# Where VectorE and ScalarE do the work between two matmul jobs: the convolution's weight sums, the feed-forward's norm, retention's gates

## The chip, the cores and the metric

The kernel is one program on one core of one Trainium2 chip. It computes one inference step of a small two-layer decoder. The metric is the device time of one execution in microseconds (us); smaller is better. The engines are named as the profile names them: PE (TensorE, matrix products), PEld (its weight loads), DVE (VectorE), ACT (ScalarE), POOL (GpSimd) and SP (SyncE, which issues most of the loads).

## The reference

Two groups of tokens share all weights: a prompt of 512 tokens and 8 sample sequences of 4 tokens, together 544 columns. D_MODEL is 1024, D_FF is 2816. Layer 0 mixes with a short gated convolution, layer 1 with four heads of retention; each layer then has a feed-forward. All is float32.

```python
def rmsnorm(x, g):
    return x * rsqrt(mean(x * x) + RMS_EPS) * g

def swiglu(x, w_gate, w_up, w_down):
    return (silu(x @ w_gate) * (x @ w_up)) @ w_down

def short_conv_mixer(x, buf, w_in, w_conv, w_out):
    b, c, h = split(x @ w_in, 3)
    u = c * h
    full = concatenate([buf, u], axis=1)
    y = sum(w_conv[j] * full[:, j:j + L] for j in range(3))
    return (b * y) @ w_out, full[:, -2:]

def retention_mixer(x, s0, pos, w_in, gn_g, w_out):
    q, k, v, g = split(x @ w_in)
    o, S = retention_chunkwise(rotary(q, pos), rotary(k, pos) * 256 ** -0.5, v, s0)
    return (silu(g) * groupnorm(o) * gn_g) @ w_out, S

for i in range(2):
    x = x + mixer_i(rmsnorm(x, norm_mix[i]))
    x = x + swiglu(rmsnorm(x, norm_ffn[i]), w_gate[i], w_up[i], w_down[i])
y = rmsnorm(x, final_norm)
```

The outputs are y of both groups, the last two rows of the convolution's input, and the retention states S.

## The kernel before

**Operands.** Every float32 operand of a matmul is split into a high part and a low part of a narrower type: `split` makes the high part on ACT (L202) and the low part on DVE (L203). A product is high x high, high x low and low x high. Names show it: `wh` and `wl` are the parts of a weight, `h` and `l` those of a sum. The activations `x` lie with features on the 128 partitions and tokens along the row, 544 columns in two halves of 272 (`HT`).

**Jobs.** Where two blocks of outputs use the same activations, the kernel computes a 2 x 2 block product with seven products instead of eight (a Strassen scheme). One such unit is a `Job`. Its products run in the order 1, then 6, 5, 2 in some turn, then 7, 3, 4; each is 12 matmuls of 272 columns (four blocks of depth by three split products, L411; a feed-forward's `down` has three blocks). Products accumulate in PSUM banks `a`, `b`, `c`: 1, 6, 7 and 4 run on in the same bank `a`, so that between them the bank is read out: `summed` takes product 1 as "u1", 6 as "u2" and 5 as "p5" with copies on ACT (L514), and adds "c11", "u3" and "c12" on DVE (L516). The "u3" add, after product 7, is called the third sum. "c21", after product 4, is taken by the job's own function.

**Weights of a job.** `weights7` loads two weights of 128 x 1024 (tiles `w`, SP's queue) and makes from them four sums of 128 x 512 on DVE (L357 to L360: two into `w2`, one in place, one into `w4`). Then the parts: of the first and the third weight by `mixed` (ACT L333 high part, DVE L334 half of the low part, ACT L335 a negated copy into the other half, and a POOL DMA L336 that adds the weight to it from DRAM), of `w2` and `w4` by `split` (`h2`, `l2`, `h4`, `l4`). The tiles `w`, `wh` and `wl` come from pools of three, those of `w2` and `w4` from single ones; `cb` is one large buffer that serves as a second `w`.

**Order.** `run` goes through a list of jobs: it prepares the next job's weights in the code ahead of the current job's middle products, starts the next job's first product, and ends the current job. A scheduler merges the code into one row of instructions for each engine; `tc.issue_after(x)` gives an instruction a place behind x in the same engine's row. Each engine runs its row in order, so an instruction that waits holds all behind it. PSUM has two double banks (`mm`) and four single ones (`sm`) in these stages.

**The four places.** The convolution (`job`, run from L735) has jobs in turn for c, h and b of two feature blocks; its first pair is computed by plain products (L187) and is scaled by the norm's factors R in L677 before the jobs start. A feed-forward (`ffn`, called once for each layer) has jobs in pairs of gate and up; while its first two run, the norm's factor is made: five small matmuls (L274), DVE L249, POOL's power L252, five transposes on PE (L256) and copies into R on ACT (L285, L286). Gate's result is copied (L871), multiplied by R (DVE L872), goes through Silu (ACT L873) and is multiplied by R again. Retention's `gates` (run inside the first feed-forward's last part through `ahead`, 583 to 686 us) has eight gate jobs and three k jobs. A gate job ends in c21: a copy on ACT (L1168), a product with R on DVE (L1170), Silu on ACT (L1171), two scales on ACT (L1173), and a store of the tile to DRAM from ACT's queue (L1174). The tile is one of the four of tag "gu".

## Time and profile before

| | us |
|---|---|
| device time, three runs | 1387.44, 1388.99, 1385.43 |
| median | 1387.44 |
| profiled execution, its own time | 1386.94 |
| its span in the trace | 1385.2 |
| granted clock of TensorE, mean | 0.999 |

The profile names an instruction by its line, its engine, its operation and its tiles (output <- inputs, buffer numbers left out). A row of a timeline reads: start in us from the span's start, duration in us, engine, line, operation, out<-in, size, count, and in brackets the time for which the engine stood idle ahead of it, with what released it. The table of stretches gives for each window its length, and for each engine the busy time and the count of instructions, then the granted clock, the DMA share and the bytes moved. In the groups by tile three numbers in ns are the shortest, the median and the longest. PE's matmuls overlap, so the sum of busy times of neighbours is more than the time from start to start.

### The profile page before, as it was taken

Reading aid. Unit: us, or ns where it says so; the run is one execution under the profiler, and the core shown is the slowest. Engines: PE = TensorE matmul, PEld = TensorE weight load, DVE = VectorE, ACT = ScalarE, POOL = GpSimd, SP = SyncE. Lnnn points to the kernel's source line nnn. Section 1 sums busy time; section 2 is a strip of 40 time slices with the busy share of each in tenths; the row PEclk is TensorE's granted clock in tenths of the full one; section 3 lists DMA queues with packets and bytes.
Section 4 is the critical chain, followed back from the end, with each engine's and each line's share of the span. In section 5 each row is a group of like instructions: output and inputs, shape, how many; then the busy total and the mean of one; then the engine's idle time right before and its main releaser. Section 6 shows DMA issues by size and latency. Waiting matters only on the chain.

```text
span 1385.2 us, 26505 instructions
## 1 busy us (share of the span) xinstructions
PE 1375.7 (99%) x10420; PEld 1313.7 (95%) x10420; DVE 1134.0 (82%) x1929; ACT 822.9 (59%) x1288; POOL 217.8 (16%) x249
## 2 busy tenths in 40 slices
PE   9999999999999999999999999999999999999998
PEld 9999999999999999999978887887899999999997
DVE  6988889898989888777868586586799898989875
ACT  7666567667667656767641413224377767667654
POOL 0111011212222213211200000000112212221212
PEclk9999999999999999999999999999999999999999
DMA  6477347777777754777666455475756777777752
GB/s 224 115 162 169 109 107 162 176 169 179 151 184 154 165 126 123 201 175 221 187 230 228 149 186 201 136 261 183 220 131 157 171 176 173 155 178 166 165 111 88
DMA packets 99438, 232.89 MB, mean 168 GB/s; under 512 B 9809, under 2 KB 33889, under 8 KB 98929
## 3 DMA queue, kind: packets, MB, share of 16 engines
q1 hardware_dynamic: 68464, 167.26, 39.2%
q0 software_dynamic: 28400, 55.82, 23.4%
q10 hardware_dynamic: 2448, 8.12, 1.5%
q8 instruction: 81, 1.33, 0.4%
q14 instruction: 45, 0.36, 0.1%
HBM read 191.05 MB, written 28.42 MB: 158 GB/s over the span
## 4 chain that ended last, share of the span: by engine, by line
PE 94%; DVE 3%; ACT 1%; DMA 1%; issue 0%; POOL 0%; DVEq 0%; SPq 0%; POOLq 0%; ACTq 0%
PE sm L411 43%; PE mm L411 16%; PE mm L187 14%; PE sm L187 5%; PE sm L1344 2%; PE sm L1345 2%; PE sm L1346 2%; PE sm L175 2%; PE sm L176 1%; PE sm L177 1%; PE sm L1594 1%; DVE ol L203 1%; DMA w<-in_cvin_dram 1%; PE mm L1355 1%; PE mm L1612 1%; PE mm L1522 1%
## 5 line engine op out<-in xcount | busy, mean ns | idle before, releaser
L411 PE MATMUL sm<-oh,wh 128*128 128x272 f32 x856 | 247.2, 289 | 1.3 <-DVE h L516 1.3
L411 PE MATMUL sm<-ol,wh 128*128 128x272 f32 x856 | 246.2, 288 | 0.0
L411 PE MATMUL sm<-oh,wl 128*128 128x272 f32 x856 | 246.1, 288 | 0.0
L202 ACT ACTIVATE h<-w 128x512 fp32r<-128x512 f32 (+3 forms) x171 | 137.7, 805 | 85.8 <-PE mm L411 77.6
L203 DVE TENSOR_TENSOR l<-w,h 128x512 fp32r<-128x512 f32 (+3 forms) x171 | 154.6, 905 | 23.2 <-ACT h L202 21.0
L333 ACT ACTIVATE wh<-w 128x1024 fp32r<-128x1024 f32 (+1 forms) x133 | 132.9, 999 | 53.5 <-PE sm L411 43.4
L411 PEld LDWEIGHTS sm<-oh,wh 128*128 128x128 f32 x856 | 161.3, 188 | 1.9 <-DVE h L516 1.5
L411 PEld LDWEIGHTS sm<-oh,wl 128*128 128x128 f32 x856 | 161.0, 188 | 0.0
L411 PEld LDWEIGHTS sm<-ol,wh 128*128 128x128 f32 x856 | 160.8, 188 | 0.0
L202 ACT ACTIVATE wh<-w 128x1024 fp32r<-128x1024 f32 (+3 forms) x80 | 69.2, 874 | 123.7 <-PE mm L187 61.2
L411 PE MATMUL sm<-parts,wh 128*128 128x272 f32 x736 | 142.6, 288 | 0.0
L336 POOL DMA_DIRECT2D wl<-in_ffgu_dram x87 | 81.7, 939 | 320.5 <-ACT wl L335 136.0
L411 PEld LDWEIGHTS sm<-parts,wh 128*128 128x128 f32 x736 | 115.5, 188 | 0.0
L411 PE MATMUL mm<-oh,h 128*128 128x272 f32 x396 | 114.0, 288 | 0.0
L411 PE MATMUL mm<-oh,l 128*128 128x272 f32 x396 | 113.4, 286 | 0.0
L411 PE MATMUL mm<-ol,h 128*128 128x272 f32 x396 | 113.1, 286 | 0.0
L411 PE MATMUL sm<-parts,wl 128*128 128x272 f32 x368 | 106.3, 289 | 0.0
L335 ACT ACTIVATE wl<-wh 128x512 fp32r<-128x512 f32 (+1 forms) x172 | 102.4, 595 | 2.2
L334 DVE TENSOR_TENSOR wl<-w,wh 128x512 fp32r<-128x512 f32 (+1 forms) x133 | 86.3, 649 | 16.3 <-ACT wh L333 16.2
L203 DVE TENSOR_TENSOR wl<-w,wh 128x1024 fp32r<-128x1024 f32 (+3 forms) x80 | 81.2, 1023 | 14.0 <-ACT wh L202 13.4
L187 PE MATMUL mm<-parts,wh 128*128 128x272 f32 x488 | 82.6, 291 | 0.1
L411 PE MATMUL sm<-oh,h 128*128 128x272 f32 x284 | 82.4, 290 | 0.0
(384 smaller groups left out, 3822.4 us busy)
## 6 DMA issues: line engine op xcount, KB each, us to landing
w<-in_ffgu_dram SPq DMA_DIRECT2D x66, 512.0 KB
wl<-in_ffgu_dram POOLq DMA_DIRECT2D x87, 256.0 KB, 5.7
S<-in_rets_dram SPq DMA_DIRECT2D x16, 1024.0 KB
out_rets_dram<-S SPq DMA_DIRECT2D x16, 1024.0 KB
w<-in_ffdn_dram SPq DMA_DIRECT2D x36, 384.0 KB
cb<-in_ffgu_dram SPq DMA_DIRECT2D x22, 512.0 KB
w<-in_cvin_dram SPq DMA_DIRECT2D x21, 512.0 KB
wl<-in_ffdn_dram POOLq DMA_DIRECT2D x48, 192.0 KB, 4.8
```

The source lines that it names most:

```text
L175: nc.tensor.matmul(out, lh, rh, start=start, stop=False, skip_group_check=True)
L187: last_product[0] = nc.tensor.matmul(half(pt, hf)[:, :HT], w[:, c], act[k][:, hf * HT : (hf + 1) * HT], start=(first and k == ks[0] and i ...
L202: h = nc.scalar.activation(dh, src, AF.Copy)
L203: last_low[0] = nc.vector.tensor_sub(dl, src, dh.bitcast(F32))
L333: nc.scalar.activation(wh, w, AF.Copy)
L334: last_mixed[0] = nc.vector.tensor_sub(wl[:, :n], w[:, :n], wh[:, :n].bitcast(F32))
L335: nc.scalar.activation(wl[:, n:], wh[:, n:].bitcast(F32), AF.Copy, scale=-1.0)
L336: nc.gpsimd.dma_start(wl[:, n:], src[:, 1, :] if len(src.shape) == 3 else src[:, n:], accum_op=ALU.add)
L411: last = nc.tensor.matmul(out, w[:, c], b, start=(first and j == 0 and i == 0), stop=(j == len(self.ks) - 1 and i == 2), skip_group_check= ...
L1344: nc.tensor.matmul(out, xh[kt][:, ts_], wh[:, cw], start=(kt == 0), stop=False)
L1345: nc.tensor.matmul(out, xh[kt][:, ts_], wl[:, cw], start=False, stop=False)
L1346: last = nc.tensor.matmul(out, xl[kt][:, ts_], wh[:, cw], start=False, stop=(kt == KT - 1))
```

## The change

Nothing is computed in another way: both kernels have the same instructions, in another order on PE's helpers. There are three edits.

1. Convolution. `run` is called with a guard: from the second job on, the weight sums of the weights after next, and the splits of its first and third weight, are given a place behind the third sum of the job before. In the first pair, the four products with R (L677) stand in another order: first b's second block out of PSUM, then R squared and the two SBUF products, then c's second block.
2. Both feed-forwards. The split of the second job's fourth weight (`h4`, `l4`) is held back and issued by `rms_scale` behind the norm's DVE step; the steps in which the norm's work is woven into PE's row go from one in four to one in five, and of the empty steps behind the norm's root one is dropped (7 to 6).
3. Retention's gates. The product with R, Silu, the two scales and the store are put in a list at c21 and are issued at the next job's c11, behind the high part of the weights after it (`last_first`); after the last job the list is emptied.

The added lines shift the numbers: L333 to L336, L357 to L360, L514 and L516, L871 to L873, L1168 to L1174 of before are L335 to L338, L360 to L363, L526 and L528, L886 to L888, L1194 to L1202 of after. (L336 of after is thus L334 of before.)

```diff
-    last_low, last_minus, last_mixed = [None], [None], [None]
+    last_low, last_minus, last_mixed, last_first = [None], [None], [None], [None]
...
-    def rms_scale(sample=False, pt=None, rest=4):
+    def rms_scale(sample=False, pt=None, rest=4, then=()):
...
         rsqrt(rN[:, :n], ms[:, :n], n)
+        for made in then:
+            made()
         for _ in range(rest):
             yield
...
         nc.scalar.activation(wh, w, AF.Copy)
         last_mixed[0] = nc.vector.tensor_sub(wl[:, :n], w[:, :n], wh[:, :n].bitcast(F32))
-        nc.scalar.activation(wl[:, n:], wh[:, n:].bitcast(F32), AF.Copy, scale=-1.0)
+        minus = nc.scalar.activation(wl[:, n:], wh[:, n:].bitcast(F32), AF.Copy, scale=-1.0)
         nc.gpsimd.dma_start(wl[:, n:], src[:, 1, :] if len(src.shape) == 3 else src[:, n:], accum_op=ALU.add)
-
-    def weights7(src1, src2, sw, n, adding=False, spare=None, first=1, fourth=False, whole=False, later=()):
+        return minus
+
+    def weights7(src1, src2, sw, n, adding=False, spare=None, first=1, fourth=False, whole=False, later=(), held=None, guard=()):
...
         with ExitStack() as behind:
-            for made in later:
+            for made in (*guard, *later):
                 behind.enter_context(tc.issue_after(made.ins))
             nc.vector.tensor_add(s1, a21, a22)
             nc.vector.tensor_sub(s2, s1, a11)
...
         behind, p1, p2 = last_minus[0], parts2(2 * n), parts2(2 * n, sw, ("h2", "l2"))
-        if whole:
-            split(*p1, w1)
-        else:
-            (split_adding if adding else mixed)(*p1, w1, src1)
+        with ExitStack() as held_back:
+            for made in guard:
+                held_back.enter_context(tc.issue_after(made.ins))
+            if whole:
+                last_first[0] = split(*p1, w1)
+            else:
+                last_first[0] = (split_adding if adding else mixed)(*p1, w1, src1)
         with tc.issue_after(behind.ins) if adding else ExitStack():
             split(*p2, w2)
         p3 = parts2(2 * n)
         with ExitStack() as after:
-            for made in later:
+            for made in (*guard, *later):
                 after.enter_context(tc.issue_after(made.ins))
             mixed(*p3, w3, src2)
         p4 = parts2(n, sw, ("h4", "l4"))
-        with tc.issue_after(behind.ins) if adding else ExitStack():
-            split(*p4, w4)
+        if held is not None:
+            held.append(lambda: split(*p4, w4))
+        else:
+            with tc.issue_after(behind.ins) if adding else ExitStack():
+                split(*p4, w4)
...
-    def run(jobs, order, after, steps, ahead=False):
-
+    def run(jobs, order, after, steps, ahead=False, guard=False):
+
+        last_third[0] = None
         jobs[0].order = order
         jobs[0].begin()
         jobs[0].weave = jobs[1].weave = steps
         for i, job in enumerate(jobs):
             nxt = jobs[i + 1] if i + 1 < len(jobs) else None
             if nxt is not None:
+                if guard and last_third[0] is not None:
+                    nxt.places["guard"] = [last_third[0]]
                 nxt.prepare()
...
-    last_add = [None]
+    last_add, last_third = [None], [None]
...
                 nc.scalar.activation(first[what], src, AF.Copy)
             elif what in more:
                 last_add[0] = nc.vector.tensor_add(more[what], more[what], src)
+                if what == "u3":
+                    last_third[0] = last_add[0]
...
         pts.append(products(1, range(3), steps))
         signal(0)
+        each(lambda p, di, ri: nc.vector.tensor_mul(di, p, ri), pts[1][0], halves(b[:, 1, :]), R)
         nc.vector.tensor_mul(R2, R, R)
-        for d, r, j in ((c, R2, 1), (b, R, 0)):
-            nc.vector.tensor_mul(halves(d[:, 0, :]), halves(d[:, 0, :]), r)
-            each(lambda p, di, ri: nc.vector.tensor_mul(di, p, ri), pts[1][j], halves(d[:, 1, :]), r)
+        nc.vector.tensor_mul(halves(c[:, 0, :]), halves(c[:, 0, :]), R2)
+        nc.vector.tensor_mul(halves(b[:, 0, :]), halves(b[:, 0, :]), R)
+        each(lambda p, di, ri: nc.vector.tensor_mul(di, p, ri), pts[1][1], halves(c[:, 1, :]), R2)
...
         mixed_in(b, taps(0), 0)
-        run(jobs, (2, 5, 6), lambda i: None, iter(()), True)
+        run(jobs, (2, 5, 6), lambda i: None, iter(()), True, True)
...
             if layer == 1:
                 jobs[0].places["later"] = [residuals[5]]
+            fourth = []
+            jobs[1].places["held"] = fourth
             jobs[0].prepare(layer == 1)
...
-            steps = paced(rms_scale(rest=7), 4)
+            steps = paced(rms_scale(rest=6, then=fourth), 5)
             run(jobs, (), after, steps)
             drain(steps)
...
+        pending = []
+
+        def flush():
+            while pending:
+                with tc.issue_after(last_first[0].ins):
+                    pending.pop(0)()
...
             def gate(what, src):
                 g = tile2()
-                if what == "c21":
+                if what == "c11":
+                    flush()
+                elif what == "c21":
                     nc.scalar.activation(g[:, 1, :HT], src, AF.Copy)
-                    r = R.rearrange("p a b -> p (a b)").unsqueeze(1).to_broadcast([P, 2, T])
-                    nc.vector.tensor_mul(g, g, r)
-                    nc.scalar.activation(g, g, AF.Silu)
-                    for i in range(2):
-                        nc.scalar.activation(g[:, i, :], g[:, i, :], AF.Copy, scale=g_ret(h * 4 + n + i))
-                    nc.scalar.dma_start(gate_made[h][:, n : n + 2, :], g)
+
+                    def shaped():
+                        r = R.rearrange("p a b -> p (a b)").unsqueeze(1).to_broadcast([P, 2, T])
+                        nc.vector.tensor_mul(g, g, r)
+                        nc.scalar.activation(g, g, AF.Silu)
+                        for i in range(2):
+                            nc.scalar.activation(g[:, i, :], g[:, i, :], AF.Copy, scale=g_ret(h * 4 + n + i))
+                        nc.scalar.dma_start(gate_made[h][:, n : n + 2, :], g)
+
+                    pending.append(shaped)
 
             def k(what, src):
                 g = tile2()
-                if what == "c21":
+                if what == "c11":
+                    flush()
+                elif what == "c21":
                     nc.scalar.activation(g[:, 1, :HT], src, AF.Copy)
                     nc.scalar.dma_start(k_made[h], g)
 
...
         jobs[0].prepare()
         run(jobs, (2, 5, 6), lambda i: factors() if i == 1 else None, iter(()))
+        flush()
```

In the convolution, on DVE, where the second job's last products run: `h_68` is the pair tile of the job before, `sm_67` the bank of its third sum, `b_84` the tile of this job, `w_86`, `w_87` and `w2_88` the weights after next and their sums. Before:

```order
L358 TENSOR_TENSOR w2_88_915<-w2_88_915,w_87_914 128x512
L516 TENSOR_TENSOR b_84_855<-b_84_855,sm_85_857 128x272
L359 TENSOR_TENSOR w_86_913<-w_87_914,w_86_913 128x512
L516 TENSOR_TENSOR h_68_769<-h_68_769,sm_67_756 128x272
L360 TENSOR_TENSOR cb_67<-w_87_914,w2_88_915 128x512
L516 TENSOR_TENSOR h_68_769<-h_68_769,mm_82_815 128x272
L203 TENSOR_TENSOR l4_80_798<-w4_72_774,h4_79_797 128x512
L334 TENSOR_TENSOR wl_90_923<-w_87_914,wh_89_922 128x512
L334 TENSOR_TENSOR wl_94_933<-w_86_913,wh_93_932 128x512
L707 TENSOR_TENSOR u_104<-c_36_557,h_68_769 128x2x512
```

After:

```order
L528 TENSOR_TENSOR h_68_769<-h_68_769,sm_67_756 128x272
L360 TENSOR_TENSOR w2_88_915<-w_86_913 128x512
L528 TENSOR_TENSOR h_68_769<-h_68_769,mm_82_815 128x272
L203 TENSOR_TENSOR l4_80_798<-w4_72_774,h4_79_797 128x512
L361 TENSOR_TENSOR w2_88_915<-w2_88_915,w_87_914 128x512
L362 TENSOR_TENSOR w_86_913<-w_87_914,w_86_913 128x512
L722 TENSOR_TENSOR u_104<-c_36_557,h_68_769 128x2x512
L363 TENSOR_TENSOR cb_67<-w_87_914,w2_88_915 128x512
L336 TENSOR_TENSOR wl_90_923<-w_87_914,wh_89_922 128x512
L336 TENSOR_TENSOR wl_94_933<-w_86_913,wh_93_932 128x512
```

The third sum of `h_68`, which stood behind three of the four weight sums, now stands ahead of all four.

In retention's gates, on ACT: `gate_864` is the tile of the gate job that ends here, `gate_880` the next one's, `wh_885` to `h4_891` the parts of the weights after. Before:

```order
L333 ACTIVATE wh_885_7431<-w_882_7422 128x1024
L1168 ACTIVATE gate_864_7250<-sm_863_7237 128x272
L335 ACTIVATE wl_886_7432<-wh_885_7431 128x512
L202 ACTIVATE h2_887_7433<-w2_883_7423 128x1024
L333 ACTIVATE wh_889_7441<-cb_67 128x1024
L1171 ACTIVATE gate_864_7250<-gate_864_7250 128x1088
L335 ACTIVATE wl_890_7442<-wh_889_7441 128x512
L1173 ACTIVATE gate_864_7250<-gate_864_7250,vec_68 128x544 x2
L202 ACTIVATE h4_891_7447<-w4_884_7424 128x512
L1174 DMA gm_223_2245<-gate_864_7250 128x1088
L514 ACTIVATE gate_880_7380<-sm_879_7367 128x272
```

After:

```order
L1194 ACTIVATE gate_864_7250<-sm_863_7237 128x272
L337 ACTIVATE wl_886_7427<-wh_885_7426 128x512
L526 ACTIVATE gate_880_7380<-sm_879_7367 128x272
L202 ACTIVATE h2_887_7428<-w2_883_7418 128x1024
L526 ACTIVATE gate_880_7380<-mm_893_7459 128x272
L1199 ACTIVATE gate_864_7250<-gate_864_7250 128x1088
L335 ACTIVATE wh_889_7436<-cb_67 128x1024
L1201 ACTIVATE gate_864_7250<-gate_864_7250,vec_68 128x544
L337 ACTIVATE wl_890_7437<-wh_889_7436 128x512
L1201 ACTIVATE gate_864_7250<-gate_864_7250,vec_68 128x544
L526 ACTIVATE gate_896_7518<-sm_895_7505 128x272
L1202 DMA gm_223_2245<-gate_864_7250 128x1088
```

Two of the next job's copies (`gate_880`) now stand ahead of Silu, and the weight parts stand between Silu and the scales.

In the second feed-forward's opening, on DVE: `g_1511` is the first gate tile, `rN` the norm, `wl_1533` the low part of a weight of the third job. Before:

```order
L203 TENSOR_TENSOR l4_1522_11915<-w4_1514_11891,h4_1521_11914 128x512
L516 TENSOR_TENSOR g_1511_11887<-g_1511_11887,sm_1510_11874 128x272
L249 TENSOR_SCALAR rN_86<-mm_1527_11977 128x5
L516 TENSOR_TENSOR g_1511_11887<-g_1511_11887,sm_1523_11918 128x272
L357 TENSOR_TENSOR w2_1530_12033<-w_1528_12031 128x512
L358 TENSOR_TENSOR w2_1530_12033<-w2_1530_12033,w_1529_12032 128x512
L359 TENSOR_TENSOR w_1528_12031<-w_1529_12032,w_1528_12031 128x512
L360 TENSOR_TENSOR w4_1531_12034<-w_1529_12032,w2_1530_12033 128x512
L334 TENSOR_TENSOR wl_1533_12042<-w_1529_12032,wh_1532_12041 128x512
L872 TENSOR_TENSOR g_1511_11887<-g_1511_11887,R_85 128x1088
```

After:

```order
L528 TENSOR_TENSOR g_1511_11887<-g_1511_11887,sm_1510_11874 128x272
L249 TENSOR_SCALAR rN_86<-mm_1527_11978 128x5
L203 TENSOR_TENSOR l4_1522_11915<-w4_1514_11891,h4_1521_11914 128x512
L528 TENSOR_TENSOR g_1511_11887<-g_1511_11887,sm_1523_11916 128x272
L360 TENSOR_TENSOR w2_1530_12033<-w_1528_12031 128x512
L361 TENSOR_TENSOR w2_1530_12033<-w2_1530_12033,w_1529_12032 128x512
L362 TENSOR_TENSOR w_1528_12031<-w_1529_12032,w_1528_12031 128x512
L363 TENSOR_TENSOR w4_1531_12034<-w_1529_12032,w2_1530_12033 128x512
L887 TENSOR_TENSOR g_1511_11887<-g_1511_11887,R_85 128x1088
L336 TENSOR_TENSOR wl_1533_12042<-w_1529_12032,wh_1532_12041 128x512
```

The norm's step (L249) has moved ahead of the fourth weight's low part, and the product with R ahead of the low part of `wl_1533`. In the first feed-forward only the former moves; there the product with R stood ahead of the low part before as well.

## The prediction, made before the result was known

> **What bounds the kernel now.** I read the page's first two parts, then a table of stretches around the four places that the change touches beside an untouched one, then PE's own list of waits, then the timelines at each wait.
>
> ```profile
> span 1385.2 us, 26505 instructions
> PE 1375.7 (99%) x10420; PEld 1313.7 (95%) x10420; DVE 1134.0 (82%) x1929; ACT 822.9 (59%) x1288; POOL 217.8 (16%) x249
> ...
> core 0: us, PE busy (x) PEld busy (x) DVE busy (x) ACT busy (x) POOL busy (x), PEclk, DMA share, GB/s
> 36.00:62.00 26.00, 25.98 (x206) 25.67 (x204) 25.82 (x47) 14.23 (x21) 2.79 (x3) 1.00 0.40 92
> 62.00:76.00 14.00, 12.70 (x100) 12.37 (x99) 9.81 (x17) 10.12 (x17) 3.49 (x4) 1.00 0.88 210
> 76.00:92.00 16.00, 16.00 (x130) 16.00 (x129) 15.90 (x27) 11.38 (x21) 2.60 (x3) 1.00 0.50 112
> 190.00:210.00 20.00, 19.68 (x157) 19.23 (x156) 17.85 (x29) 15.08 (x25) 3.83 (x4) 1.00 0.43 89
> 300.00:400.00 100.00, 100.00 (x803) 100.00 (x802) 90.06 (x162) 70.59 (x110) 20.86 (x24) 1.00 0.73 166
> 584.00:624.00 40.00, 40.00 (x315) 39.38 (x314) 29.74 (x50) 27.57 (x46) 5.18 (x6) 1.00 0.72 186
> 1020.00:1046.00 26.00, 25.85 (x205) 25.41 (x205) 24.40 (x41) 19.09 (x33) 5.57 (x6) 1.00 0.57 132
> ...
> PE sm L411 <- DVE h L516: 1.3, 1, 1.3
> ```
>
> PE is the bound nearly everywhere. In the untouched stretch 803 matmuls fill 100 us: 0.1245 us each, so a product of 12 takes 1.49 us. The change removes no matmul; it can win only what PE now waits. PE's only long wait inside the program is the 1.3 us in the convolution (the last row). Two stretches stand out on another engine: VectorE (DVE) is busy 25.82 of 26 us before that wait and 15.90 of 16 us after it.
>
> The room is better read from the weight loads (PEld), which every matmul of the untouched stretch keeps at 100.00: missing are 0.33 and 1.63 us in the convolution, 0.77 in the first feed-forward's opening, 0.62 in the gates, 0.59 in the second one's opening, together 3.94 us or 0.28%. The Trainium skill says the same of the two shares (Perfetto Trace Analysis, Identifying the Most-Contended Engine): matmul busy time is a poor measure, since matmuls overlap, and the load share a better one. The rows here agree: the 584 to 624 stretch is 100% busy by PE and 39.38 of 40 by its loads. By the rule over the whole page the room would be 71.5 us (1385.2 less 1313.7), which is not what this change can reach.
>
> **The convolution's guard.** The new order lets DVE read the third sum out of PSUM before the four sums of the weights after next.
>
> ```profile
> 67.89 0.29 PE L411 MATMUL mm<-parts,l 128*128 128x272 f32 x1
> 69.47 0.39 PE L411 MATMUL sm<-oh,wh 128*128 128x272 f32 x1 [1.30 <-DVE h L516]
> ...
> 65.06 0.69 DVE L357 TENSOR_TENSOR w<-w 128x512 f32<-128x512 f32 x1
> 67.43 0.69 DVE L358 TENSOR_TENSOR w<-w,w 128x512 f32<-128x512 f32 x1 [1.68 <-DMA w<-in_cvin_dram]
> 68.99 0.43 DVE L516 TENSOR_TENSOR h<-h,sm 128x272 f32<-128x272 f32 x1
> 75.30 1.23 DVE L203 TENSOR_TENSOR l<-w,h 128x1024 fp32r<-128x1024 f32 x1 [0.96 <-ACT h L202]
> ...
> 69.07 0.61 ACT L202 ACTIVATE h<-w 128x512 fp32r<-128x512 f32 x1
> ...
> 85.55 0.68 DVE L334 TENSOR_TENSOR wl<-w,wh 128x512 fp32r<-128x512 f32 x1
> ...
> 86.35 0.33 PE L411 MATMUL sm<-parts,wl 128*128 128x272 f32 x1
> ```
>
> Now DVE stands in L358 for a weight that lands at 67.43, and the sum at 68.99, behind it, holds the next product: PE starts it at 69.47, 1.58 after its predecessor, 1.46 more than one matmul. In the new order the sum runs as soon as the seventh product is out, near 67.4 to 67.9, and PE goes on at 68.0. That 1.46 is the upper end. But what is late next is DVE itself. It now waits, in order, for the third sum (to 67.4), then for the low half l4 of a weight whose high half ACT ends at 69.68, and the two sums, u and the two low halves follow: L360 67.9 to 68.5, a sum to 68.9, l4 69.7 to 70.3, L361 and L362 (0.6 apart) to 71.5, u (1.2) to 72.7, L363 0.6, u's rest 0.2, two low halves 1.2, to 74.8. So l2, at 75.30 in the row, starts near 74.85: DVE gains 0.45. From there to 86.23, where the low half of the next job's first weight ends, the row of 76 to 92 has no idle to give, and PE's matmul at 86.35 already comes just behind it. PE, 1.46 ahead, meets that instruction only 0.45 ahead. I take 0.45; ends 0 and 1.46. The load behind the later low halves is the next cover: it starts some 2.6 us later (71.57 to 74.2), and L361 of that job wants it near 82, 7.8 us on. The rows show no landing time for it; the bound is that nothing is lost below 7.8 us of flight.
>
> The reordered products with R in the convolution's first pair free two PSUM banks earlier.
>
> ```profile
> 37.48 0.89 PE L187 MATMUL sm<-parts,wh 128*128 128x272 f32 x4
> ...
> 36.90 0.78 DVE L677 TENSOR_TENSOR b<-sm,R 128x272 f32<-128x272 f32 x2
> 61.38 1.28 DVE L334 TENSOR_TENSOR wl<-w,wh 128x512 fp32r<-128x512 f32 x2
> ...
> 62.11 0.39 PE L411 MATMUL sm<-parts,wl 128*128 128x272 f32 x1
> ```
>
> PE's four matmuls at 37.48 take 0.89 instead of some 0.66 and start late, waiting for the two b products; about 0.4 us. DVE does the same work in the same total, and at 62.11 PE waits for the first of the two low halves of 61.38, which no earlier PE moves. I count 0; ends 0 and 0.4.
>
> **The first feed-forward's opening.** The norm's five small matmuls start one step later, the held split of the fourth weight goes behind the norm's DVE step.
>
> ```profile
> 197.85 0.29 PE L411 MATMUL sm<-oh,wl 128*128 128x272 f32 x1
> 198.28 0.35 PE L274 MATMUL mm<-cb,sqacc 128*128 128x1 f32 x2
> 204.48 0.29 PE L411 MATMUL sm<-oh,wl 128*128 128x272 f32 x1
> 204.94 0.76 PE L256 MATMUL mm<-cb,rN 128*128 128x128 f32 x5 [0.18 <-POOL rN L252]
> ...
> 202.84 0.69 DVE L203 TENSOR_TENSOR l<-w,h 128x512 fp32r<-128x512 f32 x1 [1.07 <-ACT h L202]
> 203.45 0.16 DVE L249 TENSOR_SCALAR rN<-mm 128x5 f32<-128x5 f32 x1
> ...
> 203.69 1.20 POOL L252 TENSOR_TENSOR rN<-rN,expo 128x5 f32<-128x5 f32 x1 [2.04 <-DVE rN L249]
> ```
>
> Before 198.28 and 204.94 PE gives 0.43 and 0.46 where 0.125 is due: 0.30 and 0.34. Three further matmuls (0.37) cover the first. L249 no longer sits behind L203, which idles 1.07; it can run near 201.8, POOL's 1.20 ends near 203.2, before PE arrives. 0.64 at most, 0.3 if one fails; DVE has a tenth of idle in the rows that follow (90.06), so I take 0.6.
>
> **The gates.** Silu, two scales and the store move from a job's last product to the next job's c11, behind the first split of the weight after. Per gate job, from the view of tile gate:
>
> ```profile
> L1173 ACT ACTIVATE gate<-gate,vec x14: 732/737/752, 584.9 to 680.6; 128x544 f32<-128x544 f32 x14
> L1171 ACT ACTIVATE gate<-gate x7: 1098/1107/1115, 583.0 to 678.6; 128x1088 f32<-128x1088 f32 x7
> ```
>
> 2.58 us (1.107 and twice 0.737) that ACT does later, with no operation more or fewer. ACT is busy 27.57 of 40 there, so nothing is bought but time for the splits. PE's order becomes the plain one of seven whole products; the fillers between 584 and 624 go, and with them up to 0.62. A weight that PE frees at the end of one product is wanted again four products (6 us) later, where a split costs ACT and DVE some 2.3. At the end, DVE has a full low half (1.2) ahead of the last job's third sum, about 0.3 late. The store leaves later behind Silu; its tile is one of four in turn, wanted again three jobs on. I take 0.4; ends minus 0.5 and 0.62.
>
> **The second feed-forward's opening** has the same edits but another order behind them.
>
> ```profile
> 1039.16 0.68 DVE L334 TENSOR_TENSOR wl<-w,wh 128x512 fp32r<-128x512 f32 x1
> 1039.98 1.29 DVE L872 TENSOR_TENSOR g<-g,R 128x1088 f32<-128x1088 f32 x1
> ...
> 1036.20 0.40 ACT L514 ACTIVATE u<-sm 128x272 f32<-128x272 f32 x1 [0.99 <-PE sm L411]
> 1042.24 1.12 ACT L873 ACTIVATE g<-g 128x1088 f32<-128x1088 f32 x1
> ```
>
> The product with R (1.29) now precedes the low half of 1039.16, and the copy of 1036.20 now follows Silu and one more split. From R near 1039.0: g's product to 1040.7, the low half to 1041.35, while PE wants it near 1041.1; Silu to 1042.1, the split to 1043.1, the copy to 1043.4, PE wanting it near 1043.0. That is 0.25 and 0.45 lost, against 0.4 won at the norm's matmuls and the sum now placed ahead of a split: minus 0.3; ends minus 0.9 and 0.59.
>
> **The sum:** 0.45 + 0 + 0.6 + 0.4 - 0.3 = 1.15 us. Against the profiled execution, 1386.94 (span 1385.2), that is 1385.8; the median of the runs, 1387.44, lies 0.5 above it, so 1386.3 on its scale. I say 1386.2.
>
> **The rivals.** All the room is won: 1387.44 less 3.94 is 1383.5, less than 0.3% (4.2 us, about what a measurement of this kernel can tell from no change). For it: each edit sits at one of the waits. Against it: DVE's 15.90 of 16. Chance 0.16, half of it beyond 0.3% by the runs' scatter.
>
> The gain is eaten: DVE holds PE as before in the convolution, and the second feed-forward's loss is its 0.9; with the load's flight over 7.8 us more than that. 1387.5 to 1390. Chance 0.18. For it: the two near ties above.
>
> Slower: in ACT's queue the moved 2.58 stands ahead of the next job's copies. A copy of the sixth product is wanted two products (2.99 us) later by the seventh. If one split (1.05) comes with it, 3.63 is more than 2.99 and PE waits 0.64 in each of eight gate jobs: 5.1 us, less the other places' 0.75: 1391.8. It decides at 0.4 us of other work in between. Against it: in the new order's rows that copy mostly stands ahead of Silu. Chance 0.08.
>
> **How the numbers follow.** My forecast, 1384.5 to 1387.4, has 0.58. Faster by over 0.3%: 0.08, half of the first rival. Slower: 0.08, the last. Within: 0.84. The range 1383.3 to 1389.6 leaves out the last rival, half of the first and the far end of the second.
>
> **What would show it.** PE's 1.3 us wait on DVE h gone, and a wait of 0.5 to 1 us at the next job's first low half (86 us) in its place; PE straight through 198 and 204; PEld of the gates near 100%; small new waits near 1041 and 1043. A wait repeating each gate job, or the convolution's loads landing late, would make me wrong to the slow side; a convolution 1.4 us shorter at 92, to the fast one.

## The result, and the profile after

The changed kernel takes 1384.64 us (median of 18 runs, 1383.44 to 1387.12), the kernel before 1387.36 in 18 runs beside it (1385.43 to 1390.06). The ratio is 0.9979, with a 95% interval from 0.9972 to 0.9985: 2.7 us or 0.2% less. On a second chip, as a control in the experiments, it was 0.9987 (0.9978 to 0.9996): 1385.62 against 1387.08, 1.5 us less. 1386.2 had been forecast, 1.2 us less.

The first two parts of the page after, the same stretches as before with the place near 108 us added, and PE's list of waits:

```profile
span 1382.4 us, 26518 instructions
PE 1374.0 (99%) x10420; PEld 1312.6 (95%) x10420; DVE 1133.8 (82%) x1929; ACT 822.9 (60%) x1288; POOL 212.6 (15%) x249
...
36.00:62.00 26.00, 26.00 (x210) 25.84 (x208) 25.82 (x46) 14.27 (x21) 2.80 (x3) 1.00 0.40 92
62.00:76.00 14.00, 14.00 (x112) 13.97 (x112) 11.10 (x19) 11.32 (x20) 3.49 (x4) 1.00 0.79 179
76.00:92.00 16.00, 16.00 (x129) 15.85 (x128) 15.71 (x26) 11.00 (x19) 3.15 (x4) 1.00 0.66 159
105.00:115.00 10.00, 9.70 (x77) 9.48 (x77) 9.82 (x15) 7.44 (x15) 1.73 (x2) 1.00 0.53 141
190.00:210.00 20.00, 20.00 (x163) 19.96 (x162) 18.63 (x29) 15.32 (x26) 3.84 (x4) 1.00 0.47 105
584.00:624.00 40.00, 40.00 (x320) 39.84 (x319) 30.69 (x51) 27.80 (x47) 6.06 (x7) 1.00 0.70 192
1020.00:1046.00 26.00, 25.97 (x206) 25.47 (x205) 24.46 (x41) 17.79 (x31) 4.72 (x5) 1.00 0.61 146
...
PE mm L187 <- DVE parts L222: 0.3, 1, 0.3
PE sm L420 <- DVE b L528: 0.3, 1, 0.3
```

The 1.3 us wait on DVE `h` is gone: weight loads (PEld) now fill 13.97 of the 14 us from 62 to 76. The openings of the first feed-forward (19.96 of 20) and the gates (39.84 of 40) are almost without gaps. What is new is a wait on DVE `b` in a stretch that the prediction did not look at, 105 to 115 us. The wait on `parts` is at the kernel's start, 12 us, where nothing was changed.

Since both kernels issue the same 10,420 matmuls, in almost the same order, their times can be laid over each other: for each stretch, the time between two matmuls of PE's row less the time between the same two in the kernel before. The columns are in us of the kernel before; the rows of the experiments, told below, are shown with it.

| stretch | 1-34 | 34-40 | 66-71 | 71-80 | 80-92 | 105-115 | 190-215 | 580-630 | 630-690 | 850-960 | 1018-1050 |
|---|---|---|---|---|---|---|---|---|---|---|---|
| the change | +0.46 | -0.46 | -1.52 | 0 | +0.15 | +0.50 | -0.77 | -0.63 | +0.27 | -0.60 | -0.06 |
| the change, control | +0.57 | -0.41 | -1.53 | +0.68 | +0.14 | +1.13 | -0.76 | -0.63 | +0.27 | -0.07 | -0.05 |
| guard alone | -0.03 | -0.30 | -1.51 | 0 | +0.15 | +1.35 | 0 | 0 | 0 | -0.62 | 0 |
| gates alone | +0.54 | -0.10 | +0.27 | 0 | 0 | +0.12 | 0 | -0.63 | +0.27 | -0.40 | 0 |
| norm alone | +0.43 | -0.17 | +0.10 | 0 | 0 | +1.21 | -0.76 | -0.08 | 0 | -0.61 | -0.04 |
| products with R alone | +0.69 | -0.41 | -0.24 | 0 | 0 | +0.52 | 0 | +0.15 | 0 | +0.12 | 0 |
| change without guard | +0.72 | -0.41 | -0.45 | 0 | 0 | +0.21 | -0.76 | -0.63 | +0.26 | -0.41 | -0.05 |

Two columns hold what no edit touches and still differ by 0.7 us and more from run to run: the start, and 850 to 960 (retention's chunks). Of the 2.77 us between the two profiled executions, 0.60 lies in the latter and is no gain of this change, as the 0.46 at the start is no loss of it. Other columns come out the same, within 0.05, in every run with their edit. And three do not: 71-80 and 105-115 differ between the two runs of the changed kernel, 66-71 between kernels that are alike there. The experiments explain them.

### The profile page after: what moved, and what is told of

It reads as the page before. It is cut to its first block, busy times and chain, and to the rows that moved or that the text cites. A ratio compares the mean times of both kernels' runs of the same rounds, so it can differ in the third digit from the quotient of the medians.

```text
span 1382.4 us, 26518 instructions
## 1 busy us (share of the span) xinstructions
PE 1374.0 (99%) x10420; PEld 1312.6 (95%) x10420; DVE 1133.8 (82%) x1929; ACT 822.9 (60%) x1288; POOL 212.6 (15%) x249
## 4 chain that ended last, share of the span: by engine, by line
PE 97%; DVE 1%; DMA 1%; ACT 0%; issue 0%; POOL 0%; SPq 0%; DVEq 0%; ACTq 0%; POOLq 0%
PE sm L420 44%; PE mm L420 16%; PE mm L187 16%; PE sm L187 5%; PE sm L1377 2%; PE sm L1379 2%; PE sm L1378 2%; PE sm L175 2%; PE sm L176 1%; PE sm L177 1%; PE sm L1627 1%; DMA x<-in_xT_dram 1%; PE mm L1388 1%; PE mm L1645 1%; PE mm L1555 1%; DMA w<-in_cvin_dram 0%
## 5 line engine op out<-in xcount | busy, mean ns | idle before, releaser
L335 ACT ACTIVATE wh<-w 128x1024 fp32r<-128x1024 f32 (+1 forms) x133 | 132.8, 999 | 52.6 <-PE sm L420 40.3
L338 POOL DMA_DIRECT2D wl<-in_ffgu_dram x87 | 81.9, 941 | 323.6 <-ACT wl L337 136.9
L336 DVE TENSOR_TENSOR wl<-w,wh 128x512 fp32r<-128x512 f32 (+1 forms) x133 | 86.3, 650 | 13.4 <-ACT wh L335 13.2
```

The lines of the kernel that those rows point to most:

```text
L335: nc.scalar.activation(wh, w, AF.Copy)
L336: last_mixed[0] = nc.vector.tensor_sub(wl[:, :n], w[:, :n], wh[:, :n].bitcast(F32))
L338: nc.gpsimd.dma_start(wl[:, n:], src[:, 1, :] if len(src.shape) == 3 else src[:, n:], accum_op=ALU.add)
```

## The experiments

Times are medians of 11 runs; "before" is measured beside them on the same chip.

### The four parts alone

Each kernel is the kernel before with one part of the change. The diffs are those pieces of the change; for the guard, for example, its code and

```diff
-        run(jobs, (2, 5, 6), lambda i: None, iter(()), True)
+        run(jobs, (2, 5, 6), lambda i: None, iter(()), True, True)
```

> The kernel before with the convolution's guard alone; all else as before. The prediction's theory: PE's 1.46 us at 68 us goes, DVE wins only 0.45 by the next job's low halves, PE is held near 86 us for about 1.0 us, so 0.45 us net: 1386.9 (against 1387.36). The theory from the trace of the changed kernel: PE loses only 0.15 to 0.2 near 85 us, and 0.46 near 108.6 us, where VectorE's third sum comes late because a weight lands only 1.0 us earlier; 0.9 us net by 115 us: 1386.5. A third: the load moves by the whole 1.5 us when nothing else is changed, and nothing is lost near 108.6: 1386.0. Stages behind 120 us show no change under all three.

> The kernel before with the late Silu, scales and store of retention's gates alone. The prediction's theory: 0.4 us less on PE between 584 and 686 us, nothing elsewhere: 1386.95. The rival: the 0.55 us that the changed kernel is ahead from 905 to 920 us, a stage that no edit touches, comes from here (stores that leave later or another order of transfers), then this kernel shows it too, and is 0.95 us ahead at the end: 1386.4. If 905 to 920 us agrees with the kernel before, the 0.55 is another edit's or is scatter of that stage.

> The kernel before with the held fourth split and the slower pace of the norm in both feed-forwards alone. The prediction's theory: 0.6 us won between 190 and 210 us, 0.3 lost between 1020 and 1046 us: 1387.05. The theory from the trace of the changed kernel: 0.7 us won in the first, 0.1 in the second: 1386.55.

> The kernel before with the reordered products with R of the convolution's first pair alone. The prediction's theory: 0.4 us won at 37 us and lost again at 62 us, where PE waits for the first low half of the job's weight: 1387.4. The rival: VectorE's row up to 62 us is shorter by idle time that PE's earlier products remove, and the 0.4 stays: 1387.0. Under the first, PE's wait before the matmul at 62 us grows from 0.18 to about 0.5 us; under the second it stays.

Measured: the guard 1386.07, ratio 0.9990 (0.9981 to 0.9998); gates 1387.07, 0.9999 (0.9990 to 1.0008); norm 1386.99, 0.9998 (0.9990 to 1.0007); products with R 1387.83, 1.0004 (0.9994 to 1.0013); before 1387.11. With intervals of 1.2 us on each side, times can't tell parts of 0.4 us. The table can: the gates are worth 0.63 less 0.27 in every run, as forecast; the first norm 0.76; the second 0.04, where a loss was forecast. The 0.6 of 850 to 960 us also turns up with the guard alone and with the norm alone, and the control, which is the changed kernel itself, has only 0.07 of it; so it belongs to no edit.

The products with R were forecast to win 0.4 at 37 us and lose it at 62. They lose nothing at 62: PE's wait before the low half there was 0.18 in this run, as before. What they win depends on more than the edit. In the kernels without it, PE's wait near 37 us was 0.42, 0.32, 0.24 and 0.12, in step with DVE's idle time for a weight's landing just ahead (0.45, 0.34, 0.27, 0.16 us). The last of the four is the guard alone:

```profile
33.46 0.69 DVE L361 TENSOR_TENSOR w<-w,w 128x512 f32<-128x512 f32 x1 [0.16 <-DMA w<-in_cvin_dram]
36.58 0.78 DVE L691 TENSOR_TENSOR b<-sm,R 128x272 f32<-128x272 f32 x2
...
37.27 0.78 PE L187 MATMUL sm<-parts,wh 128*128 128x272 f32 x4
```

With the edit, the two products that free the banks stand ahead of the SBUF products; they ran at 34.94 in the changed kernel, and PE's four matmuls of 37.73 took the plain 0.66. That trace alone does not tell the edit from the load, for DVE did not stand for the weight in it, nor in that of the products with R alone. The later runs with the edit do: in the control, the change without the guard and the last experiment DVE stood 0.30, 0.31 and 0.37 us for it, and PE still lost at most 0.01. The edit removes whatever wait the load left, 0.1 to 0.4.

The guard alone shows all three moving columns: it wins 1.51 at 68 us and loses 1.35 near 108, at a place that the guard hardly changes. The norm alone loses 1.21 there too, and it has no edit in the convolution. So the loss is not the guard's.

### Is it the load, VectorE's row, or the transfer beside it?

In the changed kernel, the timelines of DVE and PE near 108 us (load issued at 95.58, its landing in DVE's bracket; the time between the two, 3.79 us here, is called its flight):

```profile
95.58 0.33 SPq L354 DMA_DIRECT2D w<-in_cvin_dram  x1
...
99.37 0.69 DVE L361 TENSOR_TENSOR w<-w,w 128x512 f32<-128x512 f32 x1 [2.87 <-DMA w<-in_cvin_dram]
...
107.98 0.80 DVE L645 SCALAR_TENSOR_TENSOR y<-u,vec,y 128x560 f32<-128x560 f32 x1
108.69 0.43 DVE L528 TENSOR_TENSOR b<-b,sm 128x272 f32<-128x272 f32 x1
...
109.18 0.39 PE L420 MATMUL sm<-oh,wh 128*128 128x272 f32 x1 [0.30 <-DVE b L528]
```

DVE stands 2.87 us for a weight; behind it the row is full until the third sum at 108.69, for which PE waits. Four kernels on the changed one try this: the taps of y moved behind that third sum; the norm's two halves apart, as more looks at the same place; and the changed kernel without the 544 KB transfer of y's low half that is under way when the load starts.

```diff
-                    pair["y"] = taps(f, (0,))
+                    pair["y"] = taps(f, ())
...
-                        second_taps(f, pair["y"], 1)
+                        for row in range(2):
+                            second_taps(f, pair["y"], row)
```

> The changed kernel, with the first two taps of the convolution's y (VectorE, 0.8 us each) issued behind the third sum of their job; the same instructions. In the row of the job at 106 us the third sum then stands two taps earlier, 1.4 us. If PE's wait at 108.6 us (0.46 in the changed kernel, 1.31 with the guard alone) comes from VectorE's row that starts late behind a weight's landing, it is 0 for a flight of the load up to about 4.8 us, and the kernel ends 0.5 to 1.3 us earlier: 1384.0. If VectorE is full from there to 117 us, the taps are late next: PE's wait near 117 us, 0.15 before, grows by what was won at 108.6: 1384.6. If the wait comes from PE's own operands (the low half or the weight), it stays at 108.6.

```diff
-            jobs[1].places["held"] = fourth
```

> The changed kernel without the held split of the fourth weight in both feed-forwards; the slower pace stays. The prediction's theory: the norm's VectorE step waits behind the low half again, and PE waits before the five transposes near 204 us: 0.34 us lost there and about as much near 1036 us, where the sum after it is also late; the 0.30 before the first norm matmul at 198 stays won: 1385.3. The rival: once the steps come later, the transposes also come later and meet a finished norm; nothing is lost: 1384.6. Up to 190 us this run and the next one are two more looks at the changed kernel: PE's wait at 108.6 us should be the flight of the second load (issued near 95.6 us) less 3.3 us in both.

```diff
-            steps = paced(rms_scale(rest=6, then=fourth), 5)
+            steps = paced(rms_scale(rest=7, then=fourth), 4)
```

> The changed kernel with the norm's steps at the old pace (one in four, seven empty steps), the held split stays. The prediction's theory: PE waits 0.30 us before the first small matmul near 197 us and 0.31 near 1028 us, as in the kernel before; the 0.34 before the transposes stays won: 1385.2. The rival: the held split alone takes both waits, since VectorE is ahead: 1384.6.

```diff
-            (split if f == KT - 2 else split_adding)(yhh, yll[:, f : f + 2, :], b)
+            if f == 2:
+                nc.scalar.activation(yhh, b, AF.Copy)
+                last_minus[0] = nc.scalar.activation(yll[:, f : f + 2, :], yhh.bitcast(F32), AF.Copy, scale=-1.0)
+            else:
+                (split if f == KT - 2 else split_adding)(yhh, yll[:, f : f + 2, :], b)
```

> The changed kernel without one transfer: the low half of the convolution's second y (544 KB, from SBUF to SBUF with an add, under way from 87.7 to 96.2 us) is left as the negated high half, so that later results lack that part. If the second load of 95.6 us flies longer than 3.3 us because it shares the transfer engines with what this transfer pushes back, its flight falls to 3.3 us or less and PE's wait at 108.6 us is gone: 0.5 to 1.3 us less, 1384.0. If the flight depends on something else, it is again between 3.3 and 4.6 us and so is the wait: 1384.6.

Measured, against 1386.89 before: taps 1385.78, 0.9988 (0.9979 to 0.9997); without the held split 1384.94, 0.9981 (0.9972 to 0.9990); at the old pace 1385.36, 0.9986 (0.9977 to 0.9995); without the transfer 1384.27, 0.9979 (0.9970 to 0.9987).

The taps behind the sum: PE's wait at 108 us is gone, at a flight of 4.14 us that else costs 0.8. It is paid back with more near 117 (118.40 in this trace), where PE loses 1.38 to a low half at the end of the same full row, and 0.34 near 141. Another 0.36 from 150 to 190 us lies at no wait: each matmul there takes about 1 ns longer than in the changed kernel, and nothing ties that to the edit.

```profile
108.91 2.94 DVE L645 SCALAR_TENSOR_TENSOR y<-u,vec,y 128x560 f32<-128x560 f32 x4
...
118.40 0.39 PE L420 MATMUL sm<-parts,wl 128*128 128x272 f32 x1 [1.22 <-DVE wl L336]
```

So DVE's row is the limit there, and its start is set by the load. Without the transfer, the load of 95.78 lands 2.32 us after its issue, and PE has no wait near 108. This is one trace, but 2.32 is 1.0 below the shortest flight of all the others:

```profile
95.78 0.33 SPq L354 DMA_DIRECT2D w<-in_cvin_dram  x1
...
98.10 0.69 DVE L361 TENSOR_TENSOR w<-w,w 128x512 f32<-128x512 f32 x1 [1.40 <-DMA w<-in_cvin_dram]
```

In the thirteen other profiled runs that load flew 3.31 to 4.64 us, and why it differs so much with the transfer in place stays open. In the twelve of them that keep the taps ahead of the sum, PE's wait is that flight less 3.3: 0.08 for 3.31, 0.16 for 3.49, 0.27 for 3.59, 0.46 for 3.79, 0.89 for 4.21, 1.09 for 4.41, 1.17 for 4.51, 1.31 for 4.64. Of the eight listed, three are kernels without the guard (3.31, 3.49 and 4.51). In the changed kernel, 3.9 us from the issue on are filled by 299 GB/s at a DMA share of 0.97:

```profile
95.50:99.40 3.90, 3.90 (x33) 3.90 (x33) 1.03 (x4) 1.03 (x2) 0.87 (x1) 1.00 0.97 299
```

The Trainium skill (Perfetto Trace Analysis, Engine Utilization, Roofline) gives about 435 GB/s as what a core's 16 DMA engines move together. The row is busy to 0.97 at 299 GB/s, so a share near 1 does not mean that rate here; no run shows why.

The same law holds for the load of 62 us, with the guard as the term that changes. The landing is the first instruction that waited for the weight: DVE's second sum without the guard, ACT's high part with it.

| load of 62 us | flight | PE's wait near 68 | PE's wait near 72.4 |
|---|---|---|---|
| change without guard | 4.29 | 1.02 | 0 |
| products with R alone | 4.51 | 1.23 | 0 |
| before | 4.74 | 1.46 | 0 |
| norm alone | 4.85 | 1.57 | 0 |
| gates alone | 5.00 | 1.74 | 0 |
| the change | 3.99 | 0.04 | 0 |
| guard alone | 4.18 | 0.04 | 0 |
| the change, control | 4.82 | 0.05 | 0.58 |
| without the held split | 4.93 | 0.05 | 0.67 |

Without the guard PE waits the flight less 3.27; with it, the flight less 4.25, and only at the next point where the load's chain meets PE: ACT's copy of the sixth product, which stands behind the high part of the third weight, which waits for a weight sum. In the control:

```profile
67.68 1.06 ACT L335 ACTIVATE wh<-w 128x1024 fp32r<-128x1024 f32 x1 [1.66 <-PE sm L420]
71.89 1.06 ACT L335 ACTIVATE wh<-w 128x1024 fp32r<-128x1024 f32 x1 [1.58 <-DVE w L362]
72.86 0.38 ACT L526 ACTIVATE b<-sm 128x272 f32<-128x272 f32 x1
...
73.29 0.39 PE L420 MATMUL sm<-oh,wh 128*128 128x272 f32 x1 [0.42 <-ACT b L526]
```

(The first bracket names PE; in six of the nine runs with the guard the same row names the weight's DMA, and in the control PE's products begin at 66.66 and 68.16, not near 67.68, so the landing is the reading that fits all of them.) The guard thus buys 0.98 us of slack against one load, less 0.15 near 85 us: about 0.8 for a flight over 4.25, about 0.6 for 3.99.

VectorE's row behind the load moves with the flight too. These are the low halves `l4` (128x512) and `l2` (128x1024) that the prediction put at 69.7 and 74.85, first in the changed kernel's trace (flight 3.99):

```profile
68.88 0.69 DVE L203 TENSOR_TENSOR l<-w,h 128x512 fp32r<-128x512 f32 x1
73.76 1.22 DVE L203 TENSOR_TENSOR l<-w,h 128x1024 fp32r<-128x1024 f32 x1
```

then in the control's (flight 4.82), with PE's row where it meets the next job's first low half:

```profile
69.96 0.69 DVE L203 TENSOR_TENSOR l<-w,h 128x512 fp32r<-128x512 f32 x1 [0.96 <-ACT h L202]
74.86 1.22 DVE L203 TENSOR_TENSOR l<-w,h 128x1024 fp32r<-128x1024 f32 x1
...
85.67 0.41 PE L420 MATMUL mm<-parts,h 128*128 128x272 f32 x2
86.02 0.40 PE L420 MATMUL sm<-parts,wl 128*128 128x272 f32 x1
```

The two matmuls of 85.67 stood ten places further on in PE's row of the kernel before, behind the low half's product; in all nine runs with the guard they stand ahead of it.

The norm's halves are worth about the same: without the held split PE gives 0.47 before the transposes and the opening wins 0.35 instead of 0.77; at the old pace it gives 0.44 before the first small matmul and wins 0.40.

```profile
203.69 0.29 PE L420 MATMUL sm<-oh,wl 128*128 128x272 f32 x1
204.16 0.76 PE L256 MATMUL mm<-cb,rN 128*128 128x128 f32 x5 [0.19 <-POOL rN L252]
```

In the second opening, without the held split it was 0.12 shorter than before, at the old pace 0.05 longer, with both 0.06 shorter. The loss near 1036 us that was expected without the held split did not come.

### Moving the transfer, and the change without its guard

If taking a transfer away helps one load, issuing another one later might help the load of 62 us: the add into yl of the first y goes behind a later transfer on POOL's queue. With it ran the change without the guard and the unchanged control.

```diff
+                adds.append(lambda: nc.gpsimd.dma_start(yll[:, f : f + 2, :], b, accum_op=ALU.add))
...
+                if j == 0 and what == "u3" and adds:
+                    with tc.issue_after(first_add[0].ins):
+                        adds.pop()()
```

> The changed kernel with one transfer issued later: the add into yl of the convolution's first y (544 KB, from 65 us on in the changed kernel) stands behind the low half's transfer of the job after next on POOL's queue, near 69 us. The same instructions, all computed. If PE's wait of 0 to 0.8 us near 72.4 us comes from the weight load issued at 62.6 us, which shares the transfer engines with this add and lands after 4.0 to 4.9 us, the load now lands within 3.5 us and the wait is gone in every run: against a run of the changed kernel in the same call 0 to 0.8 us less. If the transfer only moves onto the loads of 73.3 and 73.9 us, these are wanted by VectorE near 80.5 and 81.3 us, and PE waits there or near 85 us by more than 0.15. If the load's flight has another cause, the wait near 72.4 us stays as in the control run.

> The changed kernel without the convolution's guard. By the local prices of the runs so far, the rest of the change is worth 0.3 (products with R) + 0.77 (first norm) + 0.36 (gates) + 0 (second norm) = 1.4 us: 1385.7. If the guard is worth what its run alone gave by time (1.0 us), the changed kernel is 1.0 below this one. If the edits depend on each other (the guard gains only with the earlier products with R, or the other way round), this kernel is within 0.5 of the changed one or more than 1.8 above it.

> The changed kernel once more, unchanged, as a control on the same chip as the two others, and to tell scatter from effect. If the waits near 72.4 us (0 to 0.8) and 108.6 us (0.3 to 1.3) follow the flights of the two loads issued near 62.6 and 95.6 us, this run has both waits again with 1 us per us of flight: no wait near 72.4 for a flight of 4.0 us, 0.7 to 0.8 for 4.9; at 108.6 the flight less 3.3. The stages from 850 to 960 us and up to 34 us may differ by 0.5 us with nothing changed. Time 1384.6, within 0.6.

Measured, against 1387.08 before: late add 1386.00, 0.9988 (0.9979 to 0.9997); without the guard 1385.68, 0.9991 (0.9982 to 1.0000); control 1385.62, 0.9987 (0.9978 to 0.9996).

The add left at 69.88 instead of 65.24, and the load of 62.54 still landed after 4.79 us (4.82 in the control). So this flight is not the add's doing, and why it is 4.0 in one run and 4.9 in the next stays open. The packets of the DMA trace hold a hint. In every run one 16 KB packet of the queue named `instruction` falls into this load. In the four runs where it starts 0.33 to 0.41 us behind the issue, the load flew 3.99 to 4.51 us; in the ten where it starts 0.86 to 2.67 us behind it, 4.74 to 5.80. But no run moves that packet, and for the load of 96 us its place sorts nothing (start 1.12, flight 3.49; start 0.46, flight 4.64), so a cause is not shown.

Nor did the add only move its harm onto the next loads: VectorE did not wait for those of 74.0 and 74.6 us. The later add costs something that nobody had named: its source is a buffer that ACT wants again, and ACT then waits for it.

```profile
76.07 1.42 ACT L655 ACTIVATE y<-u,vec 128x560 f32<-128x560 f32 x2 [1.34 <-DMA yl<-b]
...
78.07 0.39 PE L422 MATMUL sm<-oh,wh 128*128 128x272 f32 x1 [0.35 <-DVE b L530]
86.71 0.40 PE L422 MATMUL sm<-parts,wl 128*128 128x272 f32 x1 [0.36 <-DVE wl L337]
```

Here 71-80 was 1.26 and 80-92 was 0.60 longer than in the kernel before (0.68 and 0.14 in the control). By time, the change without the guard and the change are level on this chip, which is what the expectation had for edits that depend on each other, and the four parts alone sum to 0.5 us less than before and not to 2.7; with 1.2 us of interval on either side of each, neither says much. In the profiled executions the control drew a flight of 4.41 near 108 and the kernel without the guard one of 3.49: 0.92 us, as much as the guard is worth. The columns of the parts are those of the whole, so nothing in the traces points to their depending on each other; that the guard shortens the time rests on its own run's 0.9990 (0.9981 to 0.9998) and on the table, and this chip's times do not show it.

### One copy ahead of one split

The last run swaps two rows of ACT in the changed kernel: the copy that PE waits for at 72.4 goes ahead of the high part.

```diff
+            if guard:
+                third_held.append(lambda: mixed(*p3, w3, src2))
...
-                nc.scalar.activation(first[what], src, AF.Copy)
+                copied = nc.scalar.activation(first[what], src, AF.Copy)
+                if what == "u2" and third_held:
+                    with tc.issue_after(copied.ins):
+                        third_held.pop()()
```

> The changed kernel with one swap in ScalarE's row, in the convolution: the copy of a job's sixth product stands ahead of the high part of the third weight of the weights after next, behind which it stood and which waits for a weight sum of VectorE. The same instructions. In the runs with the guard PE's wait near 72.4 us was the flight of the load of 62.6 us less 4.25 (0 for 4.0 and 4.2, 0.5 to 0.7 for 4.8 to 4.9). If the copy alone holds PE, that wait is gone for any flight up to 5 us, and the job from 66 to 92 us is 0.5 to 0.7 shorter than in the control run: 1385.0 against its 1385.6. If VectorE's row, which is full from 69 to 86 us, is late next by the same load, the wait comes back near 85.8 us as 0.6 to 0.8 in place of 0.2: 1385.6. For a flight under 4.25 us the two theories say the same, nothing.

Measured: 1384.33 against 1387.07 before, 0.9979 (0.9970 to 0.9988). The profiled execution drew the longest flight of all, 5.80 us:

```profile
68.79 1.06 ACT L335 ACTIVATE wh<-w 128x1024 fp32r<-128x1024 f32 x1 [2.62 <-DMA w<-in_cvin_dram]
71.59 0.40 ACT L529 ACTIVATE b<-sm 128x272 f32<-128x272 f32 x1 [0.28 <-PE sm L423]
...
75.49 0.39 PE L423 MATMUL sm<-parts,wl 128*128 128x272 f32 x1 [0.67 <-DVE wl L336]
86.93 0.39 PE L423 MATMUL sm<-parts,wl 128*128 128x272 f32 x1 [0.35 <-DVE wl L336]
```

By the law of the guard PE would have waited 1.55 us near 72.4. It does not; it loses 1.00 from 71 to 80 us and 0.58 from 80 to 92 instead, both to low halves of VectorE. So the copy was the first meeting of the load and PE, and VectorE's full row is the next; nearly all of the wait moves there. The swap has not been timed beside the changed kernel on one chip; its ratio to the kernel before equals that of the change, and whether it is the better of the two is open.

## Why the prediction was right, and where it was wrong

The direction, and that the effect lies within 0.3%, were right, and 1384.64 lies in the range. The size was not: 1.2 us was forecast, and 2.7 and 1.5 were measured on two chips. Nor is 0.3% what a measurement of this kernel can just tell from no change: with 18 runs the interval is 0.07% to either side. By its steps:

- **The guard: 0.45 forecast, by the table about 0.8 for the usual flight and 0.6 for the shortest.** The wait at 68 us goes, as stated. The loss near 86 us comes as stated (PE on a low half at 85.08), but it is 0.15 and not 1.0. "DVE gains 0.45" took a time as fixed that hangs on the load: l4 was set behind a high half that ACT ended at 69.68 in the trace of before. With the short flight of the changed kernel's trace, `l2` ran at 73.76 in place of 75.30, 1.54 earlier. With the control's 4.82, near the 4.74 that the working started from, it ran at 74.86, where 74.85 had been put. So for a like flight VectorE's row was right, and what failed is PE's path to it. PE lost 0.58 earlier, at ACT's copy near 73, which the working did not have. And two matmuls, 0.25 us, now run ahead of the low half's product, so that PE meets the late low half with that much more work done. The control reached this product at 86.02 in place of 86.35, 0.33 earlier; it had entered the stretch 0.16 later, so 0.49 was won there, and with the 0.25 about what the table gives by 92 us (1.53 less 0.68 and 0.14, or 0.71).
- **What is late next** was said to be DVE. By the runs it is the load, then whatever its chain meets first: ACT's copy at 72.4 (0 or 0.7), then VectorE's row, as the last experiment shows. The second load of the same kind, at 95.6 us, was not in the working at all; its flight decides on 0 to 1.3 us near 108, in both kernels alike. The "over 7.8 us of flight" named the load behind the later low halves, for which VectorE did not wait in any of the fourteen profiled runs.
- **The products with R: 0 forecast, 0.1 to 0.4 measured.** The range held it. The step that failed is that no earlier PE would move the low halves of 62 us: VectorE came as much earlier as PE did, and the wait there stayed at 0.18 to 0.25.
- **The first feed-forward: 0.6 forecast, 0.77 measured**, both waits as named, and each half of the edit takes its own.
- **The gates: 0.4 forecast, 0.36 measured** (0.63 won, 0.27 lost at the end, where "about 0.3 late" had been put). The third sum behind a low half is in the trace as described, and a wait repeating in each gate job, the slower rival, did not come.
- **The second feed-forward: a loss of 0.3 forecast, a gain of 0.06 measured.** Both new waits came where they were put, but as 0.15 each and not 0.25 and 0.45. Silu was done at 1039.02, on the scale of the kernel before some 0.4 earlier than worked out, one split and the copy followed, and PE went on at 1040.30. The steps were right; the two durations of delay were mis-sized.

The terms as measured, 0.6 to 0.8, about 0.27, 0.77, 0.36 and 0.06, sum to 2.0 to 2.3 us, between the two measured differences. Four of the five came out better than forecast, so that 1384.64 is inside the forecast's own band, from 1384.5 on, by only 0.14 us; that is luck.

## What to carry to other kernels

When a wait ends on a transfer, its length in one trace is one draw of that transfer's flight; compare several traces of the place before pricing it, and price an edit as the slack it buys against the flight. After that, ask for the next meeting point of the same late data with the bound engine, since an engine whose row is full passes a delay on, and times in the trace that hang on the wait about to be removed can't be used as fixed points. To price parts of a change that are under the scatter of the times, lay the traces over each other by the matmul's place in PE's row.

## What was not expected of the hardware

The same 512 KB load in the same place took 3.99 to 5.80 us in fourteen profiled runs (the one of 62 us), and 3.31 to 4.64 in thirteen (the one of 96 us), 2.32 with one other transfer taken away. A stretch without any edit, 850 to 960 us, differs by up to 0.7 us between runs, at one wait of a few small matmuls (0 to 0.5 us near 914), at a granted clock of 1.00 throughout.
